# A hybrid decoder layer on one core: an order of loads, one of products, two merges and the unread products changed

## The chip, the core and the metric

The kernel runs on one NeuronCore of a Trainium2 chip. The core has a matrix engine (PE, TensorE; its weight loads are listed apart as PEld), a vector engine (DVE), a scalar engine (ACT), a third elementwise engine (POOL) and SP, whose queue here only issues transfers (DMAs). Every engine takes its own instructions strictly in the order in which the program gives them; they meet through semaphores. The metric is the device time of one execution in microseconds (us), the median of several; a profiled execution also leaves a trace of every instruction.

## What is computed

One layer of a decoder for a prompt of 1024 tokens and 8 single-token samples, in float32, with model width 2048. Cut to what matters here:

```
mod = silu(c) @ w_ada + b_ada;  shift, scale, gate = split(mod, 3)      # w_ada: 2048 x 6144
h   = rmsnorm(x, norm_g) * (1 + scale) + shift
z   = h @ w_in                                                          # w_in: 2048 x 8208
group A (8 groups of 128 channels): y_a = B * conv3(C * h_a) * silu(gate_a)
group B (8 heads of 128): q, k, v = silu(conv4(...)); gated delta rule in chunks:
    (1 + L) T = 1 (triangular, per chunk);  u = T (beta v - ...S);  o = q S + A u;  S = decay S + k^T u
    o = rmsnorm(o) * silu(gate_b)
out = x + gate * (concat(y_a, o) @ w_out);   y = rmsnorm(out)
```

`silu(c) @ w_ada` has only 9 rows (one prompt vector, eight samples); the two big products have 1032. The last columns of `w_in` (8192 to 8207) give the heads' decay and beta ("logits").

## The kernel before

**Tiling.** Everything stands transposed, features on the 128 partitions. The tokens are worked in two halves: half 0 has 512 columns, half 1 has 512 and the 8 samples. A product of 128 output features takes its 2048 inputs in 16 steps of 128 rows. To keep float32 accuracy, weights and inputs are each split into a rounded part and a remainder (`whi`, `wlo`; `hh`, `hl`, and `yhi`, `ylo` for the second matrix), and each step is three matmuls: `whi` with `hh`, `whi` with `hl`, `wlo` with `hh` (function `passes`, line 635). So a product of half 0 is 48 matmuls of 512 columns. They are called dense matmuls below. They come from a stream of raw weight tiles (`raw`, 4 buffers), which SP loads and ACT, POOL and DVE split.

**What sets the order.** No hardware queue reorders the products. The program is generated by a planner (`_Order`, line 90) with a cost for every operation: it keeps a clock for each engine, and a side task (a generator) is continued when the planner's time has come to it. What stands in the table `order(half)` (line 1353) sets the order of products; in it `h(i, part)` is one of the four products of head i (k, q, v, gate) and `a(i, part)` the products of group i (part 0 is two of them, parts 1 and 2 one each). Side tasks, such as the heads' recurrences, are woven into that row of products. All waits in time are the hardware's; the planner fixes only who stands behind whom.

**The ramp.** Before a product can start, `h` is needed, and for it `shift` and `scale`. The first section (lines 1428 to 1574) loads `x` (16 tiles of 256 KB), then two thirds of `w_ada` in 64 units of 512 KB through 9 buffers (`wat`, `ADA = 9`), and multiplies each unit on PE with the 9 conditioning vectors (`matvec`, 8 matmuls of 256 columns or 4 of 512 per unit of k-steps, in four column strips of 32). `steps` cuts the 16 feature tiles of `h` into groups: as soon as a group's shift and scale are known (`spread`: copy, transposes of `ev`, sums on DVE), its `h` tiles are made and the first seven products advance by these k-steps (`first_products`, woven in by `fill`). `busy(n)` issues n products of a 32x32 block of ones that nobody reads.

**The heads.** A head's task (`chain`, line 1671) transposes and norms k and q, builds the chunk matrices (`gdn_prep`), inverts the 32x32 diagonal blocks on DVE in a loop of 31 steps after two trips through DRAM (`gdn_invert`), merges the blocks to 64 and then to 128 (`gdn_apply`, lines 949 to 988) and runs the recurrence over four chunks (lines 997 to 1028): for each chunk a product with the state, one with the inverse (`Y`), an update of the state from `u2`, and the output. Merges and recurrence are small matmuls between which DVE or ACT must act. When a head's recurrence is placed, `recd` rises by one. `head` (line 1689) asks at a head's first product that `recd` be at least the number of begun heads less two, and lets the planner wait otherwise, without placing any product:

```
while recd[half] < len(queue) - 2:
    od.advance()
```

The heads are begun in the order 2, 1, 3, 4, 7, 5, 0, 6.

**The end.** The last column block of half 1 is normed (`final`, line 1818) and stored with eight transfers, four on ACT's queue and four on SP's; then `busy(144)` is issued.

Of the kernel before, what the change touches and what calls it, by code (L numbers as in the profile page):

```python
# [16 lines left out]
P = 128  # L17
D = 2048
NK = 16
# [363 lines left out]
def _trunk(ctx, tc, nc, xT, w_in, w_ada, w_out, pack, consts, vecs, csq, ssm, yT, cap, cqp, ssp, cas, cqs, sss):  # L383
    od = _Order()
    V, S, G, SY = (_Engine(od, e, k) for e, k in ((nc.vector, "V"), (nc.scalar, "S"), (nc.gpsimd, "G"), (nc.sync, "Y")))
    mm, pump = _Tensor(od, nc.tensor).mm, od.pump
# [21 lines left out]
    def ch_tile():  # L408
        return ps_g.tile([P, 512], F32, tag="ch", name="cht", bufs=2)
# [521 lines left out]
    def gdn_apply(half, h, hd, gp, done, cx, kq, yt):  # L931
# [41 lines left out]

        pp = ch_tile()
        for c in range(NC):
            mm(pp[64:128, c * 64:c * 64 + 64], dU[0:64, c, 64:128], X[0:64, c, 0:64], cost=0.06, start=True, stop=True,
               tile_position=(0, 64))
        pb = gp.tile([P, NC, 64], F32, tag="pb", name="pb", bufs=1)
        S.activation(pb[64:128], pp[64:128, :NC * 64].rearrange("p (c s) -> p c s", c=NC), AF.Copy, scale=-1.0)
        yield SOON  # L980
        py = ch_tile()
        for c in range(NC):
            mm(py[0:64, c * 64:c * 64 + 64], pb[64:128, c, :], Y[64:128, c, 64:128], cost=0.112, start=True, stop=True,
               tile_position=(64, 0))
        S.activation(Y[0:64, :, 64:128], py[0:64, :NC * 64].rearrange("p (c s) -> p c s", c=NC), AF.Copy)
        yield

# [365 lines left out]
    def order(half):  # L1353


        def h(i, *parts):
            return [("h", i, part) for part in parts or range(4)]

        def a(i, *parts):
            return [("a", i, part) for part in parts]  # L1360
        if half == 0:
            r = a(2, 2) + h(1) + a(1, 0) + h(3) + a(1, 1) + h(4) + a(1, 2) + h(7, 0) + a(3, 0) + h(7, 1) + a(3, 1)
            r += h(7, 2) + a(3, 2) + h(7, 3) + h(5) + h(0, 0) + a(4, 0) + h(0, 1) + h(6) + h(0, 2) + a(4, 1, 2)
            r += h(0, 3) + a(5, 0) + a(0, 0) + a(5, 1, 2) + a(0, 1) + a(6, 0) + a(0, 2)
            return r + a(6, 1) + a(7, 0) + a(6, 2) + a(7, 1, 2)
        r = h(2) + a(2, 0) + h(1) + a(0, 0) + h(3) + a(0, 1) + a(2, 1, 2) + a(0, 2) + a(1, 0) + h(4)
        r += h(7, 0) + a(1, 1, 2) + h(7, 1) + a(3, 0) + h(7, 2) + h(5) + h(7, 3) + a(3, 1, 2)
        r += h(0, 0) + a(4, 0) + h(0, 1) + a(4, 1, 2) + h(0, 2) + h(6) + h(0, 3)
        return r + a(5, 0, 1, 2) + a(7, 0) + a(6, 0) + a(7, 1) + a(6, 1, 2) + a(7, 2)
# [6 lines left out]
    ADA = 9  # L1376
# [13 lines left out]
            ws.add(w_out, m * P, ROWS)  # L1390


    def busy(n):

        t = ch_tile()
        for _ in range(n):
            mm(t[:32, :32], ones[:32, :32], ones[:32, :32], cost=0.047, start=True, stop=True)

    def fx_tile(name):
        return tp.tile([P, WH], F32, tag="fx", name=name, bufs=FX)  # L1400
# [28 lines left out]
    with ExitStack() as pools:  # L1429
# [1 line left out]
        wats = []  # L1431


        steps = ((0, 2), (2, 2), (4, 4), (8, 4), (12, 4))


        units = [(f, nf, s_, k, 8 // nf) for f, nf in steps for s_ in range(2) for k in range(0, NK, 8 // nf)]
# [28 lines left out]
        def fill(t, most=1000):  # L1466

            while most and od.now < t and queue and max(od.ready(hs[queue[0][0]][1], False), od.now) + 0.35 < t:
                if next(queue[0][1], True):
                    queue.pop(0)  # L1470
                most -= 1

        busy(170)
        for _ in range(4):
            load_ada()
        ws.ahead(0)
        for _ in range(4, ADA):
            load_ada()
        od.spawn(norm())
        pump()  # L1480
        def matvec(f, nf, which, then=None):


            nonlocal done, lr
            ps = tp_tile()
            fill(od.ready(ps[:], True))
            n = nf * P
            last = done + len([u for u in units if u[0] == f and u[2] in which])
            while done < last:
                few = units[done:done + (1 if nf == 1 else 2)]  # L1490
                fill(max(od.ready(wt[:], False) for wt in wats[done:done + len(few)]), 3 if nf == 1 else 5)
                for _, _, s_, k0, nk in few:
                    c = which.index(s_) * n
                    for k in range(k0, k0 + nk):
                        j = k % 4
                        mm(ps[32 * j:32 * j + 32, c:c + n], sc[:, k, :], wats[done][:, (k - k0) * n:(k - k0 + 1) * n],
                           cost=0.0575 * nf + (0.18 if k == few[0][3] else 0.0), start=(k < 4), stop=(k >= 12),
                           tile_position=(0, 32 * j))
                    wats[done] = None
                    done += 1  # L1500
                    load_ada()
                    k = done - 16
                    if 0 <= k < 48 and k % 3 == 0:
                        if lr is None:
                            lr = fx_tile("lr")[:, :256].rearrange("p (k n) -> p k n", n=16)
                        SY.dma_start(lr[:, k // 3, :], w_in[k // 3 * P:(k // 3 + 1) * P, 8192:8208])
                if then:
                    then(done)
                pump()
            return ps  # L1510
# [22 lines left out]
        def first_norm(done):  # L1533

            while len(normed) < (4 if done > few0 // 2 else 2):
                od.advance()
            if done == few0 - 2:
                busy(60)

        lr = None  # L1540
        for step, (f, nf) in enumerate(steps):
# [117 lines left out]
    for half in range(2):  # L1659
# [3 lines left out]
        with ExitStack() as pools:  # L1663
# [148 lines left out]
            else:  # L1812
# [52 lines left out]
                        od.spawn(final(0, *blocks[0]))  # L1865
                od.run(final(1, *blocks[1]))
                od.drain()
                busy(144)


# [55 lines left out]
```

## Time and profile before

| | |
|---|---|
| runs, median (lowest to highest) | 2195.76 us (2192.23 to 2196.54), 3 runs |
| the profiled execution | 2200.06 us |
| its span, first to last instruction | 2198.3 us |
| PE / DVE / ACT / POOL busy, share of the span | 98% / 57% / 38% / 38% |
| matmuls and weight loads recorded | 15045 each |
| mean granted PE clock | 0.983 of full speed |
| moved by DMA | 299.66 MB, 136 GB/s |

The busy share of PE counts a matmul from its start to its modelled end, so neighbours overlap and 98% does not mean that PE is at its peak. What a place costs is read from starts: the time from the start of one dense matmul to the next, and the gaps. The granted clock of a stretch stands in its own column (PEclk, 1.00 is full speed). The unread products of `busy` count as busy PE too. In the trace one float32 matmul of the program is two records (x340 for 170), those of the dense products are one.

### The profile page before, as it was taken

What the parts mean: (1) busy time and instruction counts of PE and PEld (TensorE: products, weight loads), DVE (VectorE), ACT (ScalarE), POOL (GpSimd) and SP (SyncE); (2) the same over time, 40 slices, a digit from 0 to 9 for tenths busy, and PEclk for the clock granted to TensorE, in tenths of its full rate; (3) what the DMA queues carried; (4) which work ended last, traced back from release to release, by engine and by line L of the source; (5) the groups of instructions that cost most, each with busy time, mean ns of one, the idle gap of its engine ahead of it and who ended that gap; (6) DMA issues with size and microseconds to landing.
All of it is one profiled execution on the core that took longest, in us unless ns stands there. A gap on an engine that the chain in (4) does not pass through costs nothing. (4 is left out here: it accounts for less than half of the span.)

```text
span 2198.3 us, 40441 instructions
## 1 busy us (share of the span) xinstructions
PE 2151.2 (98%) x15045; PEld 1883.7 (86%) x15045; DVE 1255.1 (57%) x3647; ACT 828.7 (38%) x1885; POOL 830.3 (38%) x807
## 2 busy tenths in 40 slices
PE   8999999999989999999999999999999999999998
PEld 6468777778868888778899999999999999998998
DVE  3346776676866562187133866656576487255453
ACT  3234343434434323243233334243333433244553
POOL 1223433434323334322434323444433443444454
PEclk9999999999979999999999999999999999999998
DMA  9964766996534446955445565467564455868765
GB/s 320 319 213 87 159 146 163 138 145 138 122 74 94 90 90 83 85 171 179 148 105 120 107 118 114 120 99 102 106 91 91 86 105 87 99 87 242 229 205 177
DMA packets 462502, 299.66 MB, mean 136 GB/s; under 512 B 37600, under 2 KB 421344, under 8 KB 462304
## 3 DMA queue, kind: packets, MB, share of 16 engines
q1 hardware_dynamic: 438512, 284.26, 60.2%
q10 hardware_dynamic: 23792, 12.81, 2.4%
q8 instruction: 118, 1.93, 0.3%
q14 instruction: 80, 0.66, 0.1%
HBM read 277.06 MB, written 19.94 MB: 135 GB/s over the span
## 5 line engine op out<-in xcount | busy, mean ns | idle before, releaser
L321 POOL TENSOR_TENSOR wlo<-raw,whi 128x512 fp32r<-128x512 f32 x535 | 713.2, 1335 | 1243.8 <-ACT whi L321 1077.3
L370 PE MATMUL mm<-hh,whi 128*128 128x264 f32 (+1 forms) x3008 | 971.1, 323 | 7.8 <-DVE y L321 3.8
L370 PE MATMUL mm<-hl,whi 128*128 128x264 f32 (+1 forms) x3008 | 969.4, 322 | 3.0 <-DVE hl L321 3.0
L370 PE MATMUL mm<-hh,wlo 128*128 128x264 f32 (+1 forms) x3008 | 970.9, 323 | 0.9 <-POOL wlo L321 0.9
L321 ACT ACTIVATE whi<-raw 128x512 fp32r<-128x512 f32 x672 | 418.0, 628 | 636.9 <-PE mm L370 354.4
L370 PEld LDWEIGHTS mm<-hh,whi 128*128 128x128 f32 x3008 | 569.0, 189 | 60.1 <-issue 11.1
L370 PEld LDWEIGHTS mm<-hl,whi 128*128 128x128 f32 x3008 | 569.1, 189 | 46.4 <-DVE hl L321 4.4
L370 PEld LDWEIGHTS mm<-hh,wlo 128*128 128x128 f32 x3008 | 568.7, 189 | 45.6 <-issue 4.2
L370 PE MATMUL mm<-yhi,wlo 128*128 128x512 f32 (+2 forms) x768 | 249.1, 324 | 5.9 <-DVE wlo L321 3.9
L370 PE MATMUL mm<-yhi,whi 128*128 128x512 f32 (+2 forms) x768 | 247.4, 322 | 2.8 <-ACT whi L321 2.8
L370 PE MATMUL mm<-ylo,whi 128*128 128x512 f32 (+2 forms) x768 | 247.3, 322 | 0.0
L321 DVE TENSOR_TENSOR ob<-tb,xb 128x62 f32<-128x62 f32 (+30 forms) x992 | 200.9, 242 | 7.4 <-DMA tb<-ub 7.4
L321 DVE TENSOR_TENSOR xb<-xb,ob 128x62 f32<-128x62 f32 (+30 forms) x992 | 184.6, 226 | 0.0
L321 DVE TENSOR_TENSOR wlo<-raw,whi 128x512 fp32r<-128x512 f32 x137 | 106.6, 784 | 118.3 <-ACT whi L321 115.2
L370 PEld LDWEIGHTS mm<-yhi,wlo 128*128 128x128 f32 x768 | 145.5, 189 | 20.4 <-DVE wlo L321 5.2
L370 PEld LDWEIGHTS mm<-yhi,whi 128*128 128x128 f32 x768 | 145.7, 190 | 14.6 <-ACT whi L321 3.4
L370 PEld LDWEIGHTS mm<-ylo,whi 128*128 128x128 f32 x768 | 145.7, 190 | 12.9 <-issue 1.0
L321 DVE SCALAR_TENSOR_TENSOR kq<-zr,pk,kq 128x512 f32<-128x512 f32 x96 | 103.1, 1074 | 3.4
L321 DVE SCALAR_TENSOR_TENSOR res<-mm,ga,xr 128x512 f32<-128x512 f32 (+2 forms) x48 | 27.2, 568 | 116.0 <-PE mm L370 105.9
L321 DVE TENSOR_TENSOR acc<-acc,sqt 128x512 f32<-128x512 f32 (+3 forms) x70 | 53.8, 771 | 33.1 <-ACT sqt L321 32.2
L321 DVE TENSOR_SCALAR u<-cht,sm 128x128 f32<-128x128 f32 x64 | 22.2, 348 | 67.8 <-PE cht L370 67.8
L321 DVE SCALAR_TENSOR_TENSOR rt<-cht,gt_neg,v 128x128 f32<-128x128 f32 x56 | 19.5, 349 | 70.7 <-PE cht L370 70.5
(410 smaller groups left out, 2046.6 us busy)
## 6 DMA issues: line engine op xcount, KB each, us to landing
raw<-in_w_in SPq DMA_DIRECT2D x488, 256.0 KB, 5.1
raw<-in_w_out SPq DMA_DIRECT2D x160, 256.0 KB, 3.2
wat<-in_w_ada SPq DMA_DIRECT2D x64, 512.0 KB, 7.2
gw<-in_w_ada SPq DMA_DIRECT2D x64, 256.0 KB, 6.6
tb<-ub ACTq DMA_DIRECT2D x16, 512.0 KB, 5.9
raw<-in_w_in SPq DMA_DIRECT2D x48, 128.0 KB, 6.3
sl<-in_ssm SPq DMA_DIRECT2D x12, 512.0 KB, 5.9
x1s<-in_xT SPq DMA_DIRECT2D x16, 260.0 KB, 5.6
```

The source lines that it names most:

```text
L321: r = f(*args, **kw)
L370: r = self.pe.matmul(out, lhsT, rhs, **kw)
```

## The change

Five edits. The numbers of the unread products are one budget now: `spare` holds 214, `busy` takes from it, and it is called in `matvec` for the time that the planner still expects to wait for a transfer; the calls `busy(60)` and, at the very end, `busy(144)` are gone, and the first call is 160 in place of 170. The first nine `w_ada` units are issued ahead of the first raw weights, where four of them were. The last group of four feature tiles in `steps` is two groups of two. The 16 small loads of the logit columns (`lr`) go with the last eight units, not with every third one. In half 0 group 4's first part stands ahead of head 0, and head 6 three products later. In the last merge both products (64 x 64 blocks, four chunks) are cut in two strips of 32 output rows, with their planner costs changed.

```diff
@@ gdn_apply, last merge
         for c in range(NC):
-            mm(pp[64:128, c * 64:c * 64 + 64], dU[0:64, c, 64:128], X[0:64, c, 0:64], cost=0.06, start=True, stop=True,
-               tile_position=(0, 64))
+            for q in (64, 96):
+                mm(pp[q:q + 32, c * 64:c * 64 + 64], dU[0:64, c, q:q + 32], X[0:64, c, 0:64], cost=0.06,
+                   start=True, stop=True, tile_position=(0, q))
...
         for c in range(NC):
-            mm(py[0:64, c * 64:c * 64 + 64], pb[64:128, c, :], Y[64:128, c, 64:128], cost=0.112, start=True, stop=True,
-               tile_position=(64, 0))
+            for q in (0, 32):
+                mm(py[q:q + 32, c * 64:c * 64 + 64], pb[64:128, c, q:q + 32], Y[64:128, c, 64:128], cost=0.06,
+                   start=True, stop=True, tile_position=(64, q))
@@ order(0)
-            r += h(7, 2) + a(3, 2) + h(7, 3) + h(5) + h(0, 0) + a(4, 0) + h(0, 1) + h(6) + h(0, 2) + a(4, 1, 2)
-            r += h(0, 3) + a(5, 0) + a(0, 0) + a(5, 1, 2) + a(0, 1) + a(6, 0) + a(0, 2)
+            r += h(7, 2) + a(3, 2) + h(7, 3) + h(5) + a(4, 0) + h(0, 0) + a(4, 1) + h(0, 1) + a(5, 0) + h(0, 2) + h(6)
+            r += a(4, 2) + h(0, 3) + a(0, 0) + a(5, 1, 2) + a(0, 1) + a(6, 0) + a(0, 2)
@@ busy
+    spare = [214]
+
     def busy(n):
-        t = ch_tile()
-        for _ in range(n):
-            mm(t[:32, :32], ones[:32, :32], ones[:32, :32], cost=0.047, start=True, stop=True)
+        n = min(n, spare[0])
+        if n > 0:
+            spare[0] -= n
+            t = ch_tile()
+            for _ in range(n):
+                mm(t[:32, :32], ones[:32, :32], ones[:32, :32], cost=0.047, start=True, stop=True)
@@ the ramp
-        steps = ((0, 2), (2, 2), (4, 4), (8, 4), (12, 4))
+        steps = ((0, 2), (2, 2), (4, 4), (8, 4), (12, 2), (14, 2))
...
-        busy(170)
-        for _ in range(4):
+        busy(160)
+        for _ in range(ADA):
             load_ada()
         ws.ahead(0)
-        for _ in range(4, ADA):
-            load_ada()
@@ matvec
-                fill(max(od.ready(wt[:], False) for wt in wats[done:done + len(few)]), 3 if nf == 1 else 5)
+                t = max(od.ready(wt[:], False) for wt in wats[done:done + len(few)])
+                fill(t, 3 if nf == 1 else 5)
+                busy(int((t - od.now - 0.8) / 0.05))
...
-                    k = done - 16
-                    if 0 <= k < 48 and k % 3 == 0:
+                    if done >= len(units) - 8:
...
-                        SY.dma_start(lr[:, k // 3, :], w_in[k // 3 * P:(k // 3 + 1) * P, 8192:8208])
+                        for k in range(2 * (done - len(units) + 8), min(2 * (done - len(units) + 8) + 2, NK)):
+                            SY.dma_start(lr[:, k, :], w_in[k * P:(k + 1) * P, 8192:8208])
@@ first_norm
-            if done == few0 - 2:
-                busy(60)
@@ the end
                 od.drain()
-                busy(144)
```

What this moves, at three places. On PE at the beginning of the program (`ones` 32x32 are the unread products, `sqt` and `ones,acc` the norm of `x`, `wat,sc` the units of `w_ada`, `cs,rsm` and `cs,ev` transposes), before with minus, now with plus:

```order
-L370 MATMUL cht<-ones 32x32 x170
+L370 MATMUL cht<-ones 32x32 x160
 L370 MATMUL cht<-sqt,cs 128x512 x4
+L370 MATMUL cht<-ones 32x32 x16
 L370 MATMUL tpt<-wat,sc 32x256 x8
 L370 MATMUL cht<-ones,acc 128x1 x4
-L370 MATMUL tpt<-wat,sc 32x256 x16
+L370 MATMUL cht<-ones 32x32 x17
+L370 MATMUL tpt<-wat,sc 32x256 x8
+L370 MATMUL cht<-ones 32x32 x21
+L370 MATMUL tpt<-wat,sc 32x256 x8
 L370 MATMUL cht<-cs,rsm 128x128 x4
-L370 MATMUL cht<-ones 32x32 x60
 L370 MATMUL tpt<-wat,sc 32x256 x8
 L370 MATMUL tpt<-cs,ev 128x128 x4
-L370 MATMUL tpt<-wat,sc 32x256 x16
```

The 60 unread products ahead of the first step's last units have become 54 in three places before them, and four units of the second step no longer stand ahead of the first dense matmul. The budget of 214 is used up here.

On SP's queue from the last tile of `x` on, before:

```order
L321 DMA x_116<-in_xT 128x512
L321 DMA wat<-in_w_ada 128x4x256 x4
L321 DMA raw<-in_w_in 128x2x128 x8
L321 DMA wat<-in_w_ada 128x4x256 x12
L321 DMA wat<-in_w_ada 128x2x512
L321 DMA raw<-in_w_in 128x2x128 x2
```

and now:

```order
L321 DMA x_116<-in_xT 128x512
L321 DMA wat<-in_w_ada 128x4x256 x9
L321 DMA raw<-in_w_in 128x2x128 x8
L321 DMA wat<-in_w_ada 128x4x256 x7
L321 DMA wat<-in_w_ada 128x2x512
L321 DMA raw<-in_w_in 128x2x128 x4
```

The eight first loads of raw weights now stand behind the whole first step of `w_ada` (8 units) and one unit more.

On PE in half 0, where the last merge (`X,dU`, `Y,pb`) and the recurrence of the fifth begun head (head 7) stand (`v,Y`, `u,kt`, `u,dA`, `st,kq`, `rt,Y`; `ones,acc` is the norm of half 1's `x`), before:

```order
L370 MATMUL mm<-hh,wlo 128x512
L370 MATMUL cht<-X,dU 64x64 x4
L370 MATMUL cht<-Y,pb 64x64 x4
L370 MATMUL cht<-v,Y 128x128
L370 MATMUL cht<-u_6289,kt 128x128
L370 MATMUL ot<-u_6291,dA 128x128
L370 MATMUL cht<-st_165,kq 128x128 x2
L370 MATMUL cht<-rt,Y 128x128
L370 MATMUL cht<-ones,acc 128x1 x4
L370 MATMUL cht<-ones,acc 8x1
L370 MATMUL cht<-u_6324,kt 128x128
L370 MATMUL ot<-u_6326,dA 128x128
```

and now, from the same merge on:

```order
L370 MATMUL cht<-X,dU 32x64 x8
L370 MATMUL tpt<-sp 128x256 x6
L370 MATMUL mm<-hh,wlo 128x512
L370 MATMUL mm<-hh,whi 128x512
L370 MATMUL mm<-hl,whi 128x512
L370 MATMUL cht<-Y,pb 32x64 x8
L370 MATMUL mm<-hh,wlo 128x512
L370 MATMUL mm<-hh,whi 128x512
L370 MATMUL mm<-hl,whi 128x512
L370 MATMUL mm<-hh,wlo 128x512
L370 MATMUL mm<-hh,whi 128x512
L370 MATMUL mm<-hl,whi 128x512
```

Counted from the first dense matmul, before none stands between the 1920th (ahead of `X,dU`) and the 1921st (behind the last `u,dA`), which is the first of head 6's; now 114 stand between that merge's `X,dU` (behind the 1910th) and the last `u,dA` (behind the 2024th), three to 25 of them between one small product and the next that waits for it at most places, and head 6 begins behind the 2112th. The last recurrence of half 0, of the eighth head, ended before behind the 2766th and now ends behind the 2916th; the planner asks for it (`len(done) < NH`, line 1727) behind the 3024th. In half 1 the table is the same; single rows there stand some dense matmuls earlier or later.

## The prediction

> **What bounds the kernel now.** I read the page's head first, then PE's busy time by stage, then PE's instructions in order of time wherever a stage was not solid, and last what the other queues did at those places.
>
> ```profile
> PE 2151.2 (98%) x15045; PEld 1883.7 (86%) x15045; DVE 1255.1 (57%) x3647; ACT 828.7 (38%) x1885; POOL 830.3 (38%) x807
> ```
>
> PE is the bound: the next engine is busy 57%. Almost all of the time is dense matmuls at full clock, which the change neither adds nor removes. So only places can gain where PE runs something else, waits, or has a low clock. The stages show three such places that the change touches: the first 45 us, the stretch from 614 to 645, and the last 16 us. The columns are PE, PEld, DVE, ACT, POOL busy with counts, PE clock, DMA share, GB/s:
>
> ```profile
> 30.00:40.00 10.00, 8.35 (x148) 6.87 (x148) 1.28 (x2) 0.00 (x0) 0.00 (x0) 0.70 1.07 347
> 614.30:640.00 25.70, 15.78 (x69) 12.07 (x68) 18.82 (x113) 7.08 (x18) 2.84 (x6) 0.56 0.18 48
> 2182.00:2198.30 16.30, 15.37 (x288) 15.23 (x286) 3.73 (x11) 0.38 (x1) 3.46 (x5) 0.50 0.40 131
> ```
>
> In the second row PE is busy 15.78 of 25.7 us at 0.56 of the clock; in the third it is busy with nothing but unread products.
>
> **Term 1, head 6 moved behind group 4's and others' products.** PE in order of time (start, duration, instruction, records, then the idle time before it and what ended that):
>
> ```profile
> 614.32 0.39 PE L370 MATMUL mm<-hh,wlo 128*128 128x512 f32 x1
> 614.63 0.68 PE L370 MATMUL cht<-X,dU 64*64 64x64 f32 x8
> 616.92 0.49 PE L370 MATMUL cht<-v,Y 128*128 128x128 f32 x2 [0.47 <-ACT Y L321]
> 620.34 0.80 PE L370 MATMUL cht<-u,kt 128*128 128x128 f32 x2 [2.93 <-DVE u L321]
> 625.51 1.87 PE L370 MATMUL cht<-ones,acc 128*128 128x1 f32 x8 [0.86 <-DVE acc L321]
> 631.30 1.37 PE L370 MATMUL cht<-cs,rsm 128*128 128x128 f32 x5
> ...
> 640.04 0.77 PE L370 MATMUL mm<-hh,whi 128*128 128x512 f32 x1
> ...
> 645.15 0.39 PE L370 MATMUL mm<-hl,whi 128*128 128x512 f32 x1
> ```
>
> From 614.32 to 640.04 no dense matmul starts: head 6's first product waits in the program until the fifth head's recurrence is placed. That is 25.72 us for one dense matmul's pitch. What the same small products cost when dense matmuls stand between them is seen at the next head:
>
> ```profile
> 676.42 0.38 PE L370 MATMUL cht<-u,kt 128*128 128x128 f32 x2
> 676.56 0.48 PE L370 MATMUL mm<-hh,wlo 128*128 128x512 f32 x1
> 676.88 0.39 PE L370 MATMUL mm<-hh,whi 128*128 128x512 f32 x1
> 677.11 0.40 PE L370 MATMUL mm<-hl,whi 128*128 128x512 f32 x1
> ...
> 678.04 0.39 PE L370 MATMUL ot<-u,dA 128*128 128x128 f32 x2
> 678.26 0.61 PE L370 MATMUL cht<-st,kq 128*128 128x128 f32 x4
> 678.63 0.48 PE L370 MATMUL mm<-hh,wlo 128*128 128x512 f32 x1
> ```
>
> The dense pitch is 0.23 us (676.88 to 677.11); `u,kt` takes 0.14 us of PE (676.42 to 676.56), and I take the same for `rt,Y`, `v,Y` and the last `u,dA`, which have its shape; `u,dA` with `st,kq` take 0.59 (678.04 to 678.63). One head: nine times 0.14, three times 0.59 = 3.0 us, and two merges of 0.68 = 1.4. The norm of half 1's `x` took 1.87 and 1.37 at half clock here, so about 1.7 at full clock. Together 6.1 us stay. The hole is worth 25.7 - 0.2 - 6.1 = 19.4 us. Behind it the clock is still low: from 640.04 to 645.15 stand 11 dense matmuls and four transposes, which at full clock are 11 x 0.23 + 0.4 = 2.9, so 2.2 more. That is 21.6 us. In the new order the dense matmuls between the small products are three to 25, 0.7 to 5.8 us, against DVE steps of which the longest wait here was 2.93. Some will be short, as DVE was busy 18.8 of 25.7 us in the hole; I leave 1.6 us for such waits and take **-20**. Bounds: -21.6, and -10 if half of the waits come back. Group 4's two moved products bring their 8 weight tiles earlier on SP's queue, where the DMA share was 0.18; I cost them at nothing, and head 6's come that much later.
>
> **Term 2, the end.** PE's last work, then the last two stores (two queues) and their time to landing:
>
> ```profile
> 2181.80 15.57 PE L370 MATMUL cht<-ones 32*32 32x32 f32 x288
> L321 SPq DMA_DIRECT2D out_yT<-res x1: 464/464/464, 2186.3 to 2186.3; - x1
> DMA to landing us min/median/max: 5.7/5.9/6.1
> ```
>
> The unread products end at 2197.4, 0.9 before the span's end. The last store lands at 2186.3 + 6.1 = 2192.4. Without `busy(144)` the store is last: **-5.0** (2197.4 - 2192.4), with the same 0.9 behind it; bounds -4 and -6. What hid the stores is gone, so they are now the end.
>
> **Term 3, the ramp.**
>
> ```profile
> 0.99 18.34 PE L370 MATMUL cht<-ones 32*32 32x32 f32 x340 [0.99 <-POOL nhalf L321]
> 19.26 5.90 PE L370 MATMUL cht<-sqt,cs 128*128 128x512 f32 x8
> 25.09 1.07 PE L370 MATMUL tpt<-wat,sc 128*32 128x256 f32 x16
> 26.09 1.05 PE L370 MATMUL cht<-ones,acc 128*128 128x1 f32 x8
> ...
> 32.80 5.84 PE L370 MATMUL cht<-ones 32*32 32x32 f32 x120
> 38.57 1.94 PE L370 MATMUL tpt<-wat,sc 128*32 128x256 f32 x16
> ...
> 42.27 2.86 PE L370 MATMUL tpt<-wat,sc 128*32 128x256 f32 x32
> 45.05 0.50 PE L370 MATMUL mm<-hh,whi 128*128 128x512 f32 x1
> ...
> 101.47 1.23 PE L370 MATMUL tpt<-wat,sc 128*32 128x512 f32 x4 [3.09 <-DMA wat<-in_w_ada]
> ...
> 169.01 0.40 PE L370 MATMUL mm<-hh,wlt 128*128 128x512 f32 x1
> ```
>
> SP's first three `w_ada` loads and its seventh and eighth, with their landings:
>
> ```profile
> L321 SPq DMA_DIRECT2D wat<-in_w_ada x3: 368/374/379, 12.4 to 13.7; - x3
> DMA to landing us min/median/max: 6.2/7.0/7.9
> L321 SPq DMA_DIRECT2D wat<-in_w_ada x2: 507/507/507, 25.6 to 26.2; - x2
> DMA to landing us min/median/max: 7.5/7.9/8.4
> ```
>
> The first lands at 18.6, the third at 21.6: 1.5 us apart. The eighth, the last of the first step, lands at 26.2 + 8.4 = 34.6, since eight raw loads were ahead of it; in the new order at about 18.6 + 7 x 1.5 = 29.1. But PE cannot use it then. Its own row is now 320 records of 54 ns (18.34 / 340), from 0.99 to 18.3; `sqt` to 24.1; 32 records to 25.8; units to 26.8; `ones,acc` to 27.8; 34 records to 29.6; units to 30.6; 42 records to 32.9; units to 33.9; transposes to 34.5; the last units to 35.5, or 36.4 at half clock. Before, this was 40.5 (38.57 + 1.94), so it comes 4.1 to 5.0 us sooner, and the first dense matmul with it. Against that, the four units at 42.27 no longer stand in front of it and come later, some 2.0 us at full clock. From 45.05 to the logit products at 169.01 PE's starts left few gaps besides the 3.09, so this carries through: -2 to -3. The loads of raw weights land by some 34 us, six before their use. The wait of 3.09 at 101 may go or stay; the halved last step leaves 87 dense matmuls behind the last transposes where there were 102, which matters only if the last unit is late, and PE shows no wait there. The moved `lr` loads lie beside those 87 (20 us). I take **-3**; bounds -8 (the wait and the low clock gone too) and +2 (the first dense matmuls meet a low clock, 4 us at half speed).
>
> Those fills do not hold the clock: the row of 2182 has PE busy all the time at 0.50, and 30 to 40, with 5.84 us of them, has 0.70. [...]
>
> **Term 4, the merges in strips.** 16 of them, each kind (records | busy us, mean ns of one):
>
> ```profile
> L370 PE MATMUL cht<-X,dU 64*64 64x64 f32 x128 | 10.8, 224 | 0.0
> L370 PE MATMUL cht<-Y,pb 64*64 64x64 f32 x128 | 10.8, 224 | 0.5 <-ACT pb L321 0.5
> L370 PE MATMUL cht<-xc,dU 32*32 32x32 f32 x256 | 7.0, 194 | 0.0
> ```
>
> A merge product is 8 records in 0.68 us; it becomes 16 records. At the pace of the 32 x 32 tiles (7.0 / 256 = 27 ns) they take 0.44, at that of the unread products, all in one tile (54 ns), 0.87. Over 32 products that is -7.7 to +6.1 us. Two tiles in turn are nearer to the first, but each streams 64 columns where those stream 32; I take 0.60, so **-2.5**.
>
> [...]
>
> **Half 1** gets no new table, but its rows shift by some places. Its waits on PE, the longest of which is this, can vanish or grow:
>
> ```profile
> 1512.57 0.58 PE L370 MATMUL mm<-hh,whi 128*128 128x256 f32 x1 [3.79 <-DVE y L321]
> ```
>
> I take 0, and 4 us either way.
>
> **The sum** is -20 - 5 - 3 - 2.5 = -30.5 against the profiled span of 2198.3: 2167.8. That execution took 2200.06, 4.3 above the median of 2195.76; the same 30.5 from the median give **2165**.
>
> **Rivals.** (a) Half of the hole comes back as waits of PE for DVE between the spread small products: term 1 is -10, the time 2176. For it: DVE's 18.8 of 25.7 us. Against: from 676 to 679 the same spacing shows no wait at all. (b) The strips go in turn and the ramp's first products meet the low clock: terms 3 and 4 are +2 and +6, the time 2179. For it: nothing but the fills' 54 ns and the 0.70. (c) Slower than before: the heads, put back, become the bound of half 0. Before, the eighth head's recurrence ended 258 dense matmuls (60 us) ahead of the place that asks for all heads; now 108 (25 us), less the 27 up to its last transposes. If the chain of the last three heads runs more than some 19 us behind its place, PE waits there, microsecond for microsecond; from 50 us behind, the whole gain is gone, and at 60 the time is 2206. Against: DVE is the chain's engine and has 43% of the span free. (d) Better: all lower bounds that do not hang on each other (-8 in the ramp, 0.44 per merge product): 2155.
>
> **How the numbers follow.** Forecast, 2157 to 2173: 0.60. (a) 0.14, (b) 0.10, (c) 0.04, (d) 0.12. The range 2153 to 2181 holds the forecast and most of (a), (b) and (d). A measurement of this kernel tells about 0.2% (4.4 us) from no change: faster 0.92, the same 0.04 (what of (a) and (b) comes together with a worse half 1), slower 0.04 from (c).
>
> **What would show it.** Term 1: dense matmuls all through the fifth head's recurrence, no stretch of low clock near 600 to 645. Term 2: PE's last record some 10 us before the last store lands, and the span ending about 1 us behind that. Term 3: the first dense matmul near 40 us, the logit products (169.0 before) near 166. Term 4: 16 records in 0.60 us. The forecast is wrong if PE waits more than 5 us in half 0 behind 640, above all before the last product of half 0, or if a wait for raw weights stands where the first dense matmuls are.

## The result, and the profile after

The changed kernel takes 2164.03 us (median of 4, 2161.08 to 2165.27), the kernel before beside it 2195.87 (4 runs, 2192.23 to 2196.54). The ratio is 0.9856 with a 95% interval of 0.9839 to 0.9873: 31.8 us less by the medians, where 30.5 were predicted. The profiled execution took 2164.96 us, its span is 2163.2.

The page's first rows of the changed kernel:

```profile
span 2163.2 us, 40436 instructions
PE 2116.0 (98%) x15045; PEld 1853.8 (86%) x15045; DVE 1262.9 (58%) x3646; ACT 826.3 (38%) x1885; POOL 835.9 (39%) x808
```

PE is still the bound, and its records are 15045 as before, to the last one. That is chance: 160 unread products less are 320 records less, 16 merges with two products of eight records more are 256, and the last step in two groups brings 64. This equality matters below.

Where the time went is read from PE's starts at six marks in both traces: the first logit product (the end of the ramp), the first product with `yhi` of half 0, the first logit product of half 1, the first `yhi` product of half 1, the last transposes, the span's end (differences from unrounded marks).

| stretch | before | after | difference |
|---|---|---|---|
| start to logits | 169.0 | 164.4 | -4.6 |
| half 0 | 772.9 | 757.3 | -15.6 |
| output product, half 0 | 182.5 | 180.8 | -1.7 |
| half 1 | 849.1 | 843.9 | -5.2 |
| output product, half 1 | 207.7 | 205.3 | -2.4 |
| last transposes to the end | 17.1 | 11.5 | -5.6 |
| span | 2198.3 | 2163.2 | -35.1 |

The windows of the changed kernel that answer to the three shown of before (same columns):

```profile
30.00:40.00 10.00, 5.88 (x59) 3.33 (x57) 5.96 (x12) 4.68 (x8) 1.26 (x1) 0.78 1.05 303
610.00:645.00 35.00, 34.67 (x224) 28.28 (x223) 17.40 (x52) 13.18 (x30) 13.43 (x14) 1.00 0.52 105
2152.00:2163.20 11.20, 0.15 (x1) 0.00 (x0) 3.82 (x11) 0.38 (x1) 3.46 (x5) 0.50 0.57 188
```

The hole is gone: 34.67 of 35 us busy at full clock, where 15.78 of 25.7 were at 0.56. At the end PE does nothing any more while the stores leave. In the ramp PE is idle for 4 of 10 us, which is the place looked at last below.

The ramp in order of time:

```profile
0.99 17.27 PE L370 MATMUL cht<-ones 32*32 32x32 f32 x320 [0.99 <-POOL nhalf L321]
18.19 5.55 PE L370 MATMUL cht<-sqt,cs 128*128 128x512 f32 x8
23.67 1.19 PE L370 MATMUL cht<-ones 32*32 32x32 f32 x32
...
26.77 1.26 PE L370 MATMUL cht<-ones 32*32 32x32 f32 x34
27.96 1.07 PE L370 MATMUL tpt<-wat,sc 128*32 128x256 f32 x16
28.96 1.51 PE L370 MATMUL cht<-ones 32*32 32x32 f32 x42
...
37.32 0.79 PE L370 MATMUL mm<-hh,whi 128*128 128x512 f32 x1 [2.89 <-ACT hh L321]
```

The first dense matmul starts at 37.32 (45.05 before), and a merge in strips is one row:

```profile
613.17 0.64 PE L370 MATMUL cht<-X,dU 64*32 64x64 f32 x16
613.74 0.97 PE L370 MATMUL tpt<-sp 128*128 128x256 f32 x6
```

The next instruction starts 0.57 behind it, where the whole product took 0.61 (670.50 to 671.11 before).

What half 0 still loses is in PE's waits between 300 and 900, by the tile waited for (us in total, times, longest):

```profile
PE tpt L370 <- DVE sp L321: 1.7, 3, 1.3
PE cht L370 <- DVE u L321: 1.7, 2, 1.2
PE tpt L370 <- DVE os__5402 L321: 1.5, 1, 1.5
PE cht L370 <- DVE ob L321: 1.4, 1, 1.4
```

All of them are waits of a head's small products for DVE, at 371, 422, 561 and 587 us.

### The profile page after: what moved, and what is told of

It is laid out like the page before. It is cut to its first block, busy times and chain, and to the rows that moved or that the text cites. A ratio compares the mean times of both kernels' runs of the same rounds, so it can differ in the third digit from the quotient of the medians.

```text
span 2163.2 us, 40436 instructions
## 1 busy us (share of the span) xinstructions
PE 2116.0 (98%) x15045; PEld 1853.8 (86%) x15045; DVE 1262.9 (58%) x3646; ACT 826.3 (38%) x1885; POOL 835.9 (39%) x808
## 3 DMA queue, kind: packets, MB, share of 16 engines
q1 hardware_dynamic: 442608, 284.26, 61.4%
## 5 line engine op out<-in xcount | busy, mean ns | idle before, releaser
L370 PEld LDWEIGHTS mm<-hl,whi 128*128 128x128 f32 x3008 | 568.0, 189 | 47.7 <-DVE hl L321 5.9
L321 DVE TENSOR_TENSOR ob<-tb,xb 128x62 f32<-128x62 f32 (+30 forms) x992 | 191.5, 233 | 7.0 <-DMA tb<-ub 7.0
L321 DVE TENSOR_TENSOR xb<-xb,ob 128x62 f32<-128x62 f32 (+30 forms) x992 | 195.5, 237 | 0.0
L321 ACT ACTIVATE u<-cht,sm 128x128 f32<-128x128 f32 x64 | 23.5, 367 | 99.6 <-DVE u L321 95.7
```

The lines of the kernel that those rows point to most:

```text
L321: r = f(*args, **kw)
L370: r = self.pe.matmul(out, lhsT, rhs, **kw)
```

## The experiments

Each edit is told against the kernel named. "Mean packet" is the time of a packet of queue 1, which carries nearly all loads and stores: its share on the page, times the span, times 16 engines, over its packets (before: 0.602 x 2198.3 x 16 / 438512 = 48.3 ns).

### The end alone

Against the kernel before; the products left out are the last ones, which nobody reads:

```diff
                 od.drain()
-                busy(144)
```

> The kernel before with the 144 unread products at its end left out, nothing else. Theory (the last store is what ends the kernel once they are gone): 5 us less than before (4 to 6), about 2191; the last store lands 1 to 2 us before the end. Rival (something else behind the stores takes as long as the unread products did): no change, or at most 2 us less.

Measured: 2213.87 us (6 runs), ratio 1.0095 [1.0078, 1.0112]: 21 us slower. At the end itself the gain is there, 11.1 us from the last transposes to the span's end in place of 17.1:

```profile
2207.15 0.43 PE L370 MATMUL cht<-cs,rsm 128*128 128x128 f32 x2 [1.03 <-POOL rsm L321]
```

But these transposes come 26.0 us later (2181.2 before), though not one instruction ahead of them differs. Comparing the start of each PE record with the same record before: 6.1 us are lost between 479 and 555, 14.5 between 877 and 977 (times of the kernel before). The second place in windows, first of this run and then of the kernel before (columns as above, DMA share and GB/s last):

```profile
900.00:960.00 60.00, 50.65 (x190) 35.98 (x189) 5.01 (x7) 11.09 (x19) 18.28 (x16) 0.94 0.94 67
```

```profile
900.00:930.00 30.00, 30.00 (x131) 24.23 (x130) 4.38 (x5) 5.70 (x9) 12.41 (x12) 1.00 0.99 78
930.00:960.00 30.00, 25.92 (x100) 19.14 (x99) 22.24 (x32) 16.43 (x31) 7.08 (x5) 0.94 0.56 143
```

Before, the DMA engines are full (0.99) for 78 GB/s up to 930, with PE busy throughout (30.00 of 30), and then the backlog is gone. Without the 144 products they are still at 0.94 over the whole stretch to 960, for 67 GB/s, and PE waits for the split weights:

```profile
948.92 0.50 PE L370 MATMUL mm<-hh,whi 128*128 128x512 f32 x1 [0.90 <-ACT whi L321]
950.27 0.50 PE L370 MATMUL mm<-hh,wlo 128*128 128x512 f32 x1 [0.61 <-POOL wlo L321]
955.06 0.55 PE L370 MATMUL mm<-hh,whi 128*128 128x512 f32 x1 [2.20 <-ACT whi L321]
```

The same bytes in the same packets keep the DMA engines busy longer over the whole run. Queue 1 of this run (packets, MB, share), then of before:

```profile
q1 hardware_dynamic: 438512, 284.26, 66.7%
```

```profile
q1 hardware_dynamic: 438512, 284.26, 60.2%
```

That is 54.0 ns a packet against 48.3. Sorted by size, only the 512-byte packets (366208 of them, the raw weights among them) are slower: 52.1 ns against 45.2, while those of 1024 bytes take 50.7 against 50.8. So neither the prediction's account (the end costs 5 us and nothing hangs on it) nor any rival named till then held, and the next runs ask on what the packets depend.

### The order table alone

Against the kernel before: only the two changed lines of `order(0)`.

> The kernel before with the new table of products for half 0, nothing else; the merges and their planner costs as before. Theory (the table moves head 6 and so fills the hole at the fifth head): 16 to 20 us less than before, 2176 to 2180, no stretch of low clock between 600 and 650. Rival (the table only moves the wait to another place of half 0): 10 us less or fewer, 2186 or more.

Measured: 2170.64 us (4 runs), ratio 0.9897 [0.9882, 0.9913], 22 us less. Half 0 takes 750.6 in place of 772.9, every other stretch stays within 3.5 us. The hole and its neighbourhood, and PE's waits between 300 and 900:

```profile
590.00:650.00 60.00, 58.73 (x326) 47.54 (x325) 34.65 (x93) 22.82 (x47) 24.25 (x25) 1.00 0.51 107
```

```profile
PE cht L370 <- DVE st L321: 1.1, 2, 0.9
PE cht L370 <- ACT evg L321: 0.4, 1, 0.4
PE cht L370 <- DVE rsm L321: 0.3, 1, 0.3
PE tpt L370 <- DVE os__3670 L321: 0.3, 1, 0.3
```

So the table by itself takes the whole hole (22.3; 21.6 was the bound by the rows) and brings no new wait over 1 us. What the changed kernel has of this, 15.6, is less: its four groups of waits shown above sum to 6.3 us and are not here.

### Strips with the new planner costs, old table

Against the kernel before: the edit of `gdn_apply` as in the change.

> The kernel before with the merges in two strips and their new planner costs, nothing else; the table of products is the old one. Theory as predicted (the strips save about 0.04 to 0.1 us a product and the hole is a matter of the table): 1 to 3 us less than before, the hole at the fifth head still there, 2193 to 2195. Rival (the planner, with other costs for the merges, places the fifth head's merge some 90 dense matmuls sooner, and so fills the hole without the new table): 14 to 22 us less, 2174 to 2182, no hole.

Measured: 2181.1 us (4 runs), ratio 0.9948 [0.9931, 0.9966], 11.6 us less: more than the theory's 1 to 3, less than the rival's 14 to 22, whose mechanism it shows. Half 0 is 6.1 shorter (766.8), half 1 5.0 (844.1). The fifth head's last merge stands behind 1827 dense matmuls in place of 1920 here, though the table is the old one, since the planner believes the merges to cost something else; the hole is filled (first row), and the waits have moved ahead of it (second row):

```profile
590.00:650.00 60.00, 58.40 (x350) 47.47 (x349) 38.59 (x103) 25.85 (x63) 21.47 (x24) 0.99 0.44 92
560.00:590.00 30.00, 22.25 (x90) 17.68 (x89) 19.23 (x72) 12.27 (x34) 11.18 (x10) 0.84 0.55 122
```

So the edit of the strips is at the same time an edit of the order.

### The ramp alone

The changed kernel with the old table and the old merges, and with the products at the end:

```diff
                 od.drain()
+                spare[0] = 144
+                busy(144)
```

> The kernel before with the changes of its beginning (order of loads, halved last step, logit loads last, unread products in the first step's waits), and with the 144 unread products at the end kept. Theory: 3 to 5 us less than before, 2191 to 2193; first dense matmul near 37 us, logit products near 164.5. Rival (what the beginning gains is lost again by half 1, since the planner shifts rows): within 2 us of before.

Measured: 2189.89 us (12 runs), ratio 0.9983 [0.9973, 0.9993], 1.5 to 5.9 us less, which excludes neither the theory's 3 to 5 nor the rival's 2. In the profiled run the first dense matmul starts at 40.81 and the logits come at 167.6, 1.4 sooner than before. PE has the same instructions in this ramp as in the changed kernel, whose first dense matmul came at 37.32. What differs is the granted clock, here in this run and then in the changed kernel:

```profile
30.00:35.00 5.00, 5.00 (x60) 3.15 (x61) 0.28 (x1) 0.00 (x0) 0.00 (x0) 0.51 0.96 228
```

```profile
30.00:35.00 5.00, 3.71 (x55) 2.02 (x52) 1.71 (x4) 1.60 (x3) 0.20 (x1) 1.00 1.04 257
```

Here the clock falls at 30.1 us, while the last 42 fill records run (2.14 us for them, 1.51 in the changed kernel); there it falls at 35.6. Over the four profiled runs with this ramp (also the changed kernel with 85 more products and with the old table, both below) the first dense matmul starts at 37.1 to 40.9 and the logits come at 163.1 to 167.6.

### The program's length without TensorE

Against the run on the end alone:

```diff
     G.memset(phalf[:], 0.5)
+    for _ in range(576):
+        G.eng.memset(phalf[:], 0.5)
```

> The kernel before without its 144 unread products at the end, as in the run on the end alone (2213.87 us, queue 1 busy for 66.7% of 16 engines' span where the kernel before has 60.2% for the same 438512 packets), but with 576 one-after-another memsets of GpSimd put at its start, between 1.5 and 25 us, where that engine has nothing to do: the number of instructions in the program is again that of the kernel before. Theory A (the length of the whole program shifts something on which the loads' packets depend): the share goes back to 60-61% and the time to 2188 (before less the 5 us at the end). Theory B (the length of TensorE's own stream does it): the share stays at 66-67%, the time at 2210-2217. Theory C (the products at the end themselves were needed, whatever the length): as B.

Measured: 2288.96 us (4 runs), ratio 1.0442 [1.0419, 1.0465]. Two things overlap. The memsets did not take 23 us but 93, 162 ns from one to the next on the same tile, and the clearing of `sc`, for which DVE waits, stood behind them (POOL's rows, then DVE's):

```profile
1.07 93.24 POOL L443 MEMSET phalf<- 128x8 f32 x576
94.24 0.53 POOL L321 MEMSET sc<- 128x512 f32 x1
```

```profile
94.80 0.31 DVE L321 TENSOR_TENSOR sc<-cth,pk 128x144 f32<-128x144 f32 x1 [90.49 <-POOL sc L321]
```

The first dense matmul starts at 119.01 (46.21 without the memsets): 72.8 of the 75 us. What the run was for is not touched by that: queue 1.

```profile
q1 hardware_dynamic: 438512, 284.26, 64.6%
```

0.646 x 2294.3 x 16 / 438512 = 54.1 ns, as without them, and the last transposes are 101.7 us later than before: 75.7 more than without the memsets, 72.8 of them from the start. The number of instructions in the program (40439, before 40441) is not what the loads depend on: theory A is out. B and C are left.

### More unread products, where they cost nothing

Against the changed kernel:

```diff
                 od.drain()
+                spare[0] = 85
+                busy(85)
```

> The changed kernel with 85 more unread products (170 records) behind TensorE's last transposes, at 2152-2161 us, beneath the last products' stores; nothing else moves. Mean time of a packet of queue 1 so far, from share x span x 16 / packets: 54.0 ns at 14757 TensorE records, 48.3 at 15045, 47.7 at 15077, 45.0 at 15301. Theories A and B (length): at 15215 records the mean lies at 45-47 ns and the time at 2156-2164. Theory C (only the end's products): also faster loads. If neither: 48 ns and 2164-2167.

Measured: 2163.78 us (4 runs), ratio 0.9868 [0.9852, 0.9884], as the changed kernel.

```profile
q1 hardware_dynamic: 442608, 284.26, 58.3%
```

45.5 ns at 15215 records, inside the 45 to 47 that was written down. The time did not follow: the output product of half 0 is 2.1 us shorter (178.6), half 0 the same (757.6).

### The fills at the end

Against the changed kernel: budget 160, and `busy(54)` behind the last `od.drain()`.

> The changed kernel with its 54 unread products between the first matvec's pieces taken out and put behind the last transposes (same 15045 records). [...] By the rows of the ramp (each piece waits for its load of w_ada behind the products anyway) it is 0 to 1 us shorter: 2163-2164. [...]

Measured: 2161.71 us (4 runs), ratio 0.9855 [0.9841, 0.987]. It cannot be told from the changed kernel in time, but the ramp is read from the rows:

```profile
18.19 6.22 PE L370 MATMUL cht<-sqt,cs 128*128 128x512 f32 x8
24.34 1.07 PE L370 MATMUL tpt<-wat,sc 128*32 128x256 f32 x16
25.34 1.05 PE L370 MATMUL cht<-ones,acc 128*128 128x1 f32 x8
26.33 1.93 PE L370 MATMUL tpt<-wat,sc 128*32 128x256 f32 x32
...
33.21 0.53 PE L370 MATMUL mm<-hh,whi 128*128 128x512 f32 x1 [1.99 <-ACT hh L321]
```

Without the fills the units of `w_ada` run one behind the other with no wait for a load, and the first dense matmul starts 4.1 us sooner than in the changed kernel (37.1 to 40.9 in the four runs with the fills). Nothing was there for the fills to hide. The clock, by the windows of this run:

```profile
30.00:40.00 10.00, 6.31 (x28) 3.37 (x29) 5.78 (x13) 4.59 (x8) 1.28 (x1) 0.68 1.04 311
40.00:50.00 10.00, 10.00 (x76) 6.18 (x76) 1.37 (x2) 1.56 (x3) 1.29 (x1) 0.98 1.10 310
```

It loses 3.2 + 0.2 us of clock in these 20 us; the changed kernel has 0.78 and 0.88 there, 2.2 + 1.2. The low stretch is as long with the fills as without, only later. In both runs it covers the first dense matmuls, behind waits for `hh` of 2.89 and 1.99 us that no fill bridges, so this pair alone does not tell whether fills can hold a clock.

Two other places do. At the end of the kernel before, PE is busy with unread products for 15.37 of 16.3 us at a clock of 0.50 (the row at 2182.00 in the prediction). At the start of the changed kernel the trace's first clock record stands at 21.94 us, so the 1.00 that the windows show ahead of it is not a reading; the records of `sqt` start 0.85 us apart up to there and 0.43 behind it, so the 17.27 us of unread products ahead of them had left the clock at half. In both places products of 32 x 32 kept PE busy without holding the clock at 1.00.

### The changed kernel with the old table

> The changed kernel with the order table of the kernel before (same 15045 records). The prediction's first term (the table alone fills the hole at the fifth head): 2184 (20 us back). From the run of the costs alone, whose planner places the fifth head's last merge 93 dense products earlier without the table and saves 11.6: about 2174. Rival (the costs alone do all of it): 2164.

The diff is the two lines of `order(0)` put back. Measured: 2171.73 us (4 runs, 2163.51 to 2174.32), ratio 0.9892 [0.9864, 0.9919]. So in presence of the strips' costs the table brings some 8 us, not 20; the 2174 worked out from the run of the costs was nearest. The 8 are uncertain, as one of the four runs took no longer than the changed kernel. Half 0 takes 763.1, and its waits stand ahead of the old hole, as in the run of the costs:

```profile
566.96 0.49 PE L370 MATMUL cht<-rt,Y 128*128 128x128 f32 x2 [1.96 <-DVE rt L321]
570.61 0.77 PE L370 MATMUL cht<-u,kt 128*128 128x128 f32 x2 [3.16 <-DVE ob L321]
```

### The kernel before with a longer stream

Against the kernel before: `busy(272)` for `busy(144)`.

> The kernel before with 272 unread products at its end in place of 144, all behind the last transposes, so that what runs ahead of them is unchanged, but TensorE's stream has 15301 records. Theory (the length of TensorE's stream sets the loads' packets): mean packet of queue 1 45 ns in place of 48.3, a share of 55-57%, and the last transposes come 3 to 6 us earlier than at 2181.2, since the changed kernel's came 3.8 us earlier at 15215 records. Rival (what stands ahead of the products is unchanged, so nothing moves): 48 ns and 2181. In both the 272 themselves take 29 us at 54 ns a record and end the span: 2206 to 2212 us in all.

Measured: 2208.59 us (4 runs), ratio 1.0069 [1.0049, 1.0089]. Queue 1:

```profile
q1 hardware_dynamic: 438512, 284.26, 55.9%
```

45.1 ns, as forecast. But the last transposes come at 2183.3, not 3 to 6 us earlier than 2181.2. The profiled execution was a long one, 6.6 us above the median of its runs, as that of the kernel before was 4.3 above its own; counted from the medians of the two kernels run beside each other (2208.59 and 2192.37) the transposes come some 3 us later, not earlier (an estimate, with the time behind them as profiled). The packets follow the stream, the time doesn't follow the packets in this direction.

### The strips alone, with every instruction in its old place

Against the kernel before: the strips, but at costs whose sums are the old ones (`cost=0.06 if q == 64 else 0.0`, `cost=0.112 if q == 0 else 0.0`).

> The kernel before with the strips alone, planned at costs that leave every instruction in its old place (15301 records, as the run with 272 unread products, with which its last transposes are compared). By the rows of the changed kernel (a group of 16 half records takes 0.57 us, of 8 whole ones 0.61): last transposes 1.3 us earlier than there. [...] The merges that TensorE waits for may shift it by 1 us either way. The time lies 17 us behind the last transposes, 2190-2196.

Measured: 2193.32 us (10 runs) against 2192.37 (13 runs), ratio 1.0001 [0.999, 1.0013]. Half 0 takes 774.0 us in this run and in the one with 272 products, which has the same 15301 records and the whole merges. The last transposes come at 2178.8, 4.5 earlier than there, all of it in half 1 and behind, beyond what 32 products times 0.04 us explain; counted from the medians of both kernels it is some 1.8 (an estimate, as above), near the 1.3. Against the kernel before, the strips change nothing that can be measured.

The prediction's upper end of +6, by which the strips go in turn, lies outside the interval's +2.9. But it was priced at 54 ns a record, the pace of the unread products at a clock of 0.50. At 1.00 they take 36 (1.51 us for 42 between the units), and 16 times that is 0.58, so the group's 0.57 us does not tell overlap from turns. The single records do: in the changed kernel's group at 613.17 they start in pairs 7 ns apart (613.252 and 613.259), 56 ns from one pair to the next, and a weight load for the same 64 rows starts at 613.254, 2 ns behind the first of the pair (recorded with 216 ns, its end modelled). By these starts the two strips of a pair did not run in turn here, nor did that load wait for the first of them.

### Fewer unread products at the beginning

Against the run with the fills at the end: 129 at the beginning, 85 at the end; and then 75 and 85.

> The changed kernel with 129 unread products at the beginning (of 160), none between the first matvec's pieces and 85 behind the last transposes (15045 records as before). In the run with the fills at the end ScalarE's squares waited 3.95 us for the products on sqt, which stood behind the 160. Theory (the 160 are in the way of the squares): these products start 3.3 us earlier, first dense matmul at 30 in place of 33.2, 2158-2159 us. Rival (the loads of w_ada or a lower clock behind a shorter start end the ramp): 2161-2163.

> As the run before, but 75 at the beginning: 14937 records. The ramp 3 to 5 us shorter than with 160, if squares and loads allow; the mean packet of queue 1 by the line between 54.0 ns at 14757 and 48.3 at 15045 near 50.4, which would give back 4 to 9 us: 2160-2168 us. If the length did not matter: 2156-2158.

Measured: 2160.52 us (4 runs), ratio 0.9845 [0.983, 0.986], and 2166.94 (4 runs), 0.9878 [0.986, 0.9896]. In the first the squares' products start at 14.88 in place of 18.19, and it does not help:

```profile
24.59 0.64 PE L370 MATMUL tpt<-wat,sc 128*32 128x256 f32 x8 [0.61 <-DMA wat<-in_w_ada]
26.10 0.64 PE L370 MATMUL tpt<-wat,sc 128*32 128x256 f32 x8 [0.87 <-DMA wat<-in_w_ada]
...
29.11 0.64 PE L370 MATMUL tpt<-wat,sc 128*32 128x256 f32 x8 [0.85 <-DMA wat<-in_w_ada]
...
33.03 0.79 PE L370 MATMUL mm<-hh,whi 128*128 128x512 f32 x1 [1.92 <-ACT hh L321]
```

Now the units wait for their loads, and the first dense matmul stays at 33.0: the rival, the loads of `w_ada`, is right. The second run has 14937 records, and its queue shows

```profile
q1 hardware_dynamic: 442608, 284.26, 64.5%
```

50.4 ns (0.645 x 2163.3 x 16 / 442608), as the line between the earlier runs gave it. Half 0 takes 761.7 us against 755.2 in the first: 6.5 us for three more nanoseconds.

All runs together, by TensorE's records:

| run | PE records | mean packet, ns | to the last transposes, us |
|---|---|---|---|
| the end alone | 14757 | 54.0 | 2207.2 |
| the same with 576 memsets | 14757 | 54.1 | (ramp disturbed) |
| 75 and 85 | 14937 | 50.4 | 2150.3 |
| before; table alone | 15045 | 48.3; 48.1 | 2181.2; 2153.4 |
| changed; fills at the end; old table; 129 and 85 | 15045 | 48.0; 47.6; 47.7; 47.5 | 2151.6; 2147.1; 2159.7; 2143.6 |
| ramp alone | 15077 | 47.7 | 2170.5 |
| changed with 85 more | 15215 | 45.5 | 2147.8 |
| costs alone; strips alone; before with 272 | 15301 | 45.0; 44.9; 45.1 | 2161.7; 2178.8; 2183.3 |

The mean packet falls with the number of TensorE's records (32 more, as in the run of the ramp, are within the scatter of 0.8 at one number), whether the records are unread products at the end, at the beginning, or halves of a merge; for one number it is the same within that scatter, whatever else differs. That excludes theory C (that only the products at the end matter) as it did A. It is shown that the loads' packets go with the length of TensorE's stream; why is not. What the length changes, such as where something lies in memory, no view here shows.

## Why the prediction was right, point by point

**Term 1 (the hole, -20).** The mechanism was right: dense matmuls run through the fifth head's recurrence at full clock, and the table alone takes 22.3 us of half 0. In the changed kernel it is 15.6 us, and waits of the heads' small products for DVE appear that the table alone does not have (6.3 us; 6.7 between the two half 0). The allowance of 1.6 for such waits was too small. The likely origin is the strips' new planner costs, which the prediction had priced as strips only: both runs with these costs and the old table have such waits ahead of the old hole. A run with the table and the ramp but without the costs was not made, so this is not isolated. Of the rivals (a) comes closest: part of the hole came back as waits for DVE, half as much as it said. Two readings of the rows were slightly off, in opposite directions: from 640.04 to 645.15 ten dense pitches pass, not eleven (0.2 us more to win), and `u,kt` and `st,kq` also delay the second dense matmul behind them by 0.09 (0.32 from 676.56 to 676.88 in place of 0.23), 1.1 us less to win over twelve of them.

**Term 2 (the end, -5).** Measured -5.6 between the last transposes and the span's end; the rows (products to 2197.4, last store landed at 2192.4) gave the size. What failed is that the term priced the deletion at its own place and put its effect on everything ahead of it at nothing, without a reason. Left out alone the products cost 21 us, as 288 records less make the stream shorter and the loads slower. The changed kernel was spared this because its other edits put the 15045 back; without the strips and the two groups it would have had 14725, and by the run at 14757 this term would probably have had the other sign.

**Term 3 (the ramp, -3; -8 to +2).** -4.6 to the logits in the changed kernel; the ramp's edits alone give 1.5 to 5.9 by the runs. The first dense matmul came 7.7 sooner, where 4.1 to 5.0 were worked out: the fills ran at 36 ns a record (1.51 us for 42), not at the 54 that was assumed from the start's row. That row was taken at half clock, the fills of this execution at a clock of 1.00. The size is in part luck: with the same instructions in the ramp, but the clock falling at 30 us, another run gained 1.4 to the logits. That the fills do not hold the clock was right (0.50 with PE busy for 15.37 of 16.3 us at the end of the kernel before), and taking them out of the ramp brings its first dense matmul another 4.1 sooner.

**Term 4 (the strips, -2.5).** By the rows -1.3 (32 products, 0.04 each), by the runs alone 0 with an interval of -2.2 to +2.9. The prediction's 0.60 us for 16 records was 0.57 in truth, but the whole product takes 0.61 from start to start, not the 0.68 of its busy time: the term subtracted a pitch from a duration. Its upper end had a price at the wrong clock: 54 ns is the unread products' pace at 0.50, and at 1.00 they take 36.

**Half 1 (0, 4 either way).** -5.2, just outside. The run of the costs has it too (-5.0), the old table with the new costs as well (843.7), the strips in the old order don't (849.8): it is again the planner's new costs, that reorder half 1 without a new table.

**The sum.** From -30.5 to -35.1 in the profiled executions and -31.8 by the medians. Nearer than its terms: half 0 gave 4.4 less than term 1, and the ramp 1.6, half 1 5.2 and the two output products 4.1 more, on which nothing was said. That these misses partly cancel is luck; the mechanisms of terms 1 and 2 at their own places are what the runs bear out. A check from runs that were made apart: table -22.6 (0.0103 x 2195.9), end -5.6, ramp -3.7 (0.0017 x 2195.9) sum to -31.9, which leaves the strips with their costs at nothing, as what they win in half 1 they lose in half 0. Rival (c), late heads at the end of half 0, showed no trace: the longest wait of half 0 is 1.5 us. Rival (b) fell: the strips' group takes 0.57, and though the first dense matmuls do meet the low clock (35.6 to 42.4 us), the ramp gained.

No run beats the changed kernel by more than can be told: the version with 129 and 85 has 0.9845 [0.983, 0.986], the changed kernel 0.9856 [0.9839, 0.9873].

## What to carry to other kernels

A stretch in which the bounding engine only served a chain of small operations was worth its whole length here, less those operations' pitch at full clock (of 25.7 us, with the low clock behind it, 21.6 by the rows and 22.3 measured with the table alone); that is read from starts, not from busy times. A planner's cost is an edit of the order: to price an operation, keep the order as it was and change the operation alone. Before work that nobody reads is deleted, look at how near the loads are to being late: here the loads' packets followed the length of TensorE's stream, and a deletion that was right at its own place cost more than four times its gain elsewhere (26.0 us against 6.0).

## What the runs showed that was not expected

- The mean packet of queue 1 goes with the number of TensorE's instructions in the program: 54 ns at 14757 records, 48 at 15045, 45 at 15301, over fourteen kernels. Of its sizes, the 512-byte packets are the ones that differ between the end alone and the kernel before (52.1 ns against 45.2). Slower packets cost time at once (26 us to the last transposes for 5.7 ns; 6.5 us in half 0 for three), faster ones than 48 ns gained next to none (the run with 272 products, the one with 85 more). That the loads are just hidden at 48 ns would fit this, but no run shows it.
- 576 memsets of 128 x 8 on one tile took 162 ns each on POOL; in the kernel before, the memset of `phalf` starts 40 ns behind that of `nhalf`, and that of `sc` 34 ns behind `phalf`.
- The unread 32 x 32 products ran at 54 ns a record at the start and at the end, and at 36 ns (1.51 us for 42) between the first units of `w_ada`. The clock goes with it: 0.50 at the end, half at the start by the pitch of `sqt`, 1.00 between the units. At the start of the changed kernel PE was busy with such products for 17.27 us, and the clock was still at half behind them (`sqt` 0.85 us apart, later 0.43).
